# Gate tiles of a hybrid encoder block as seven block products, with stages reordered, six modulation buffers and squares in place

## The chip, the cores and the metric

The kernel runs on one core of one Trainium2 chip. The metric is the device time of one execution in microseconds (us); the median of several runs is given, and one further execution was profiled. All shares of clock and busy time below come from that profiled execution.

## The reference

One layer, 512 tokens (SEQ), model width 2048, all in float32. Cut to what matters here:

```python
mod = jax.nn.silu(c) @ w_ada[l] + b_ada[l]                 # six vectors of 2048
sh1, sc1, gt1, sh2, sc2, gt2 = jnp.split(mod, 6, axis=-1)
a = rms_norm(h, g_pre_mix[l]) * (1 + sc1) + sh1
proj = a @ w_in[l]
q, f_fw, f_bw, i_v, o_gate, z, gate_a, gate_b = jnp.split(proj, IN_SPLIT_POINTS, axis=-1)
y_a = hgrn2_bidir(q, f_fw, f_bw, i_v, o_gate, ...) @ w_a_out[l]      # 8 heads, two scans
y_b = chunked_sgu(z, g_sgu_norm[l], w_spatial[l], b_spatial[l]) @ w_b_out[l]
merged = jax.nn.sigmoid(gate_a) * y_a + jax.nn.sigmoid(gate_b) * y_b
h = h + gt1 * rms_norm(merged @ w_o[l], g_post_mix[l])
a = rms_norm(h, g_pre_ffn[l]) * (1 + sc2) + sh2
ff = jnp.square(jax.nn.relu(a @ w_ff1[l])) @ w_ff2[l]
h = h + gt2 * rms_norm(ff, g_post_ffn[l])
```

gate_a and gate_b are 2048 columns each: 16 tiles of 128 columns each, 32 gate tiles together.

## The kernel before

**Precision.** Every float32 factor is split into a high part (a cast to fp32r on ScalarE, L174) and a low part (source minus high on VectorE, L175), and a product of two such factors is the sum of three matmuls, high by high, low by high, high by low (`mm3`, L194 to L197). A tile of 128 output columns over the model width (`proj_fm`) is thus 16 x 3 = 48 matmuls of 512 token columns. Weights arrive as tiles of 1 MB (128 x 2048) by SP's DMA queue into a ring of three buffers named raw. Early stages split them in pieces of 512 columns (four buffers for the high and four for the low parts), later stages (from L663) in pieces of 1024 (four and three).

**Seven products.** `seven` (L246) computes two weight tiles at once by a Strassen-like scheme: tokens, model width and output columns are halved, and seven products of blocks take the place of eight. Each product has eight steps of a matmul of 512 columns (the high weight with the high and low activations side by side, L238) and one of 256 (the low weight with the high activation, L239). Sums of weight blocks are made on VectorE in the raw tiles (`plus`, L244). The activation side needs seven sets of blocks (S): a11, a12, a22 and the sums v1, w2, w3, v4. It is used for 28 pairs of w_ff1 tiles; `seven_tm` is its counterpart for w_o and w_ff2, where weights are the moving operand.

**Stages, in order.** (1) x is normalised and transposed; the rows of w_ada for sc1 and sh1 are multiplied with silu(c) (`ada_tile`, one VectorE instruction over a 1 MB tile, L295), two buffers named ada; each of the 16 activation tiles is modulated, split and used at once for the values of the scan and for q. (2) Eight heads: three `proj_fm` tiles each, then a scan (`head_scan`) with a long chain on VectorE. (3) Four gate_a tiles, the split of the scan's output, the other twelve gate_a tiles with two ada tiles each (`ada_next(2)`), then w_a_out. (4) The spatial gating unit: values (w_tm), layer norm, eight groups. (5) Sixteen gate_b tiles, written to DRAM, two ada tiles each until the 64 remaining ones are done. (6) w_b_out, with gate_b read back; the sums of blocks for w_o; w_o; norms. (7) w_ff1: eight plain tiles, then 28 pairs by `seven`. The result of a pair (tile both, slot h1) is added up, passed through relu and square in a further tile r (slot m1), combined to the sums that the next matrix needs, and written to DRAM by POOL's queue (L1062 to L1068). (8) w_ff2 by `seven_tm` over seven groups; s1 in slot m1 takes its first partial product. When sixteen ada tiles of one modulation are done, `post_gain` (L666) writes its 2048 numbers to DRAM as single elements.

**Order.** The tile framework lays out the instructions of each engine in an order of its own from the program's order, the tiles that come free and a planner's costs; each engine and each queue then works strictly in its order. A tile named by a slot (a0 to a7, m0 to m3, h0, h1, v0, v1) waits until the slot's last user is done.

## Time and profile before

| | |
|---|---|
| median of 3 runs | 2751.97 us (2747.85 to 2756.64) |
| profiled execution | 2751.59 us |
| its span | 2749.9 us |
| granted TensorE clock, mean | 0.991 of full |
| instructions | 33871 |
| read from DRAM, written | 422.15 MB, 69.75 MB |

The profile gives the busy time of each engine, waits with what ended them, and for each stretch of the span the share of the DMA engines in use and the TensorE clock that was granted. Busy times of consecutive matmuls overlap, so the time of one is better read from the distance between two events a known number of matmuls apart.

### The profile page before, as it was taken

Reading aid. Unit: us, or ns where it says so; the run is one execution under the profiler, and the core shown is the slowest. Engines: PE = TensorE matmul, PEld = TensorE weight load, DVE = VectorE, ACT = ScalarE, POOL = GpSimd, SP = SyncE. Lnnn points to the kernel's source line nnn. Section 1 sums busy time; section 2 is a strip of 40 time slices with the busy share of each in tenths; the row PEclk is TensorE's granted clock in tenths of the full one; section 3 lists DMA queues with packets and bytes.
Section 4 is the critical chain, followed back from the end, with each engine's and each line's share of the span. In section 5 each row is a group of like instructions: output and inputs, shape, how many; then the busy total and the mean of one; then the engine's idle time right before and its main releaser. Section 6 shows DMA issues by size and latency. Waiting matters only on the chain.

```text
span 2749.9 us, 33871 instructions
## 1 busy us (share of the span) xinstructions
PE 2680.5 (97%) x13392; PEld 2239.6 (81%) x13392; DVE 2042.4 (74%) x2442; ACT 1217.1 (44%) x1627; POOL 125.1 (5%) x152
## 2 busy tenths in 40 slices
PE   5999999999999999999999999999998999999998
PEld 4888788888788888878779988888887888888886
DVE  6876877756553666357897888888888888888856
ACT  5433333332222332233558656565655555555542
POOL 0000000000000000010000000000000011111110
PEclk9999999999999999999999999999999999999999
DMA  8852222247754558643345443434346677778772
GB/s 319 319 205 77 77 77 77 77 148 273 237 199 139 199 202 301 187 151 135 111 170 198 159 171 137 172 134 175 134 175 251 225 215 201 203 201 229 213 239 77
DMA packets 94927, 494.10 MB, mean 180 GB/s; under 512 B 10416, under 2 KB 12464, under 8 KB 47792
## 3 DMA queue, kind: packets, MB, share of 16 engines
q1 hardware_dynamic: 69168, 413.80, 42.2%
q0 software_dynamic: 25600, 78.14, 10.8%
q8 instruction: 105, 1.72, 0.2%
q14 instruction: 54, 0.44, 0.0%
HBM read 422.15 MB, written 69.75 MB: 179 GB/s over the span
## 4 chain that ended last, share of the span: by engine, by line
PE 52%; DVE 2%; issue 1%; ACT 1%; DMA 0%; DVEq 0%; ACTq 0%; POOLq 0%
PE ps_pair L238 13%; PE ps_pair L775 8%; PE ps_pair L776 8%; PE ps_pair L774 8%; PE ps_pair L239 7%; PE ps_pair L195 2%; PE ps_pair L197 2%; PE ps_pair L196 2%; PE ps_pair L1169 1%; PE ps_pair L1170 1%; PE ps_pair L1168 1%; DVE wl L175 0%; DVE raw L244 0%; DVE hr L1160 0%; ACT wh L174 0%
## 5 line engine op out<-in xcount | busy, mean ns | idle before, releaser
L174 ACT CAST wh<-raw 128x1024 fp32r<-128x1024 f32 (+1 forms) x896 | 765.8, 867 | 1015.0 <-PE ps_mm L197 391.1
L175 DVE TENSOR_TENSOR wl<-raw,wh 128x1024 fp32r<-128x1024 f32 (+1 forms) x896 | 875.6, 991 | 379.7 <-ACT wh L174 231.7
L196 PE MATMUL ps_mm<-a,wl 128*128 128x512 f32 x1152 | 450.9, 391 | 5.4 <-DVE wl L175 5.4
L195 PE MATMUL ps_mm<-a,wh 128*128 128x512 f32 x1152 | 454.3, 394 | 0.0
L197 PE MATMUL ps_mm<-a,wh 128*128 128x512 f32 x1152 | 453.5, 394 | 0.0
L238 PE MATMUL ps_pair<-mq,wh 128*128 128x512 f32 x896 | 317.2, 397 | 0.0
L196 PEld LDWEIGHTS ps_mm<-a,wl 128*128 128x128 f32 x1152 | 217.1, 188 | 51.3 <-DVE wl L175 6.6
L197 PEld LDWEIGHTS ps_mm<-a,wh 128*128 128x128 f32 x1152 | 216.9, 188 | 46.3 <-issue 1.9
L195 PEld LDWEIGHTS ps_mm<-a,wh 128*128 128x128 f32 x1152 | 217.1, 188 | 44.5 <-issue 1.9
L239 PE MATMUL ps_pair<-mq,wl 128*128 128x256 f32 x896 | 251.8, 281 | 0.0
L244 DVE TENSOR_TENSOR raw<-raw 128x1024 f32<-128x1024 f32 (+1 forms) x156 | 237.4, 1522 | 2.8
L295 DVE SCALAR_TENSOR_TENSOR raw<-raw,c_bc 128x2048 f32<-128x2048 f32 x64 | 146.5, 2290 | 102.0 <-DMA raw<-in_w_ada_dram 102.0
L238 PEld LDWEIGHTS ps_pair<-mq,wh 128*128 128x128 f32 x896 | 168.3, 188 | 40.8
L775 PE MATMUL ps_pair<-wl,a 128*128 128x512 f32 x432 | 170.2, 394 | 4.7 <-DVE wl L175 4.7
L774 PE MATMUL ps_pair<-wh,a 128*128 128x512 f32 x432 | 169.9, 393 | 0.5 <-ACT wh L174 0.5
L776 PE MATMUL ps_pair<-wh,a 128*128 128x512 f32 x432 | 169.7, 393 | 0.0
L239 PEld LDWEIGHTS ps_pair<-mq,wl 128*128 128x128 f32 x896 | 169.3, 189 | 0.0
L238 PE MATMUL ps_pair<-w,wh 128*128 128x512 f32 x448 | 159.6, 393 | 0.0
L239 PE MATMUL ps_pair<-w,wl 128*128 128x256 f32 x448 | 126.6, 283 | 0.0
L774 PE MATMUL ps_pair<-wh,v 128*128 128x512 f32 x288 | 112.9, 392 | 6.0 <-ACT wh L174 6.0
L774 PE MATMUL ps_pair<-wh,w 128*128 128x512 f32 x288 | 113.8, 395 | 3.1 <-ACT s L1130 2.1
L775 PE MATMUL ps_pair<-wl,w 128*128 128x512 f32 x288 | 113.8, 395 | 0.8 <-DVE wl L175 0.8
(279 smaller groups left out, 4564.8 us busy)
## 6 DMA issues: line engine op xcount, KB each, us to landing
raw<-in_w_ff_dram SPq DMA_DIRECT2D x72, 1024.0 KB, 6.3
raw<-in_w_fm_dram SPq DMA_DIRECT2D x64, 1024.0 KB, 4.8
raw<-in_w_ada_dram SPq DMA_DIRECT2D x64, 1024.0 KB, 5.5
raw<-in_w_ff2s_dram SPq DMA_DIRECT2D x56, 1024.0 KB, 7.2
ada<-in_w_ada_dram SPq DMA_DIRECT2D x32, 1024.0 KB, 7.0
comb_dram<-r POOLq DMA_DIRECT2D x28, 896.0 KB, 8.6
raw<-in_w_os_dram SPq DMA_DIRECT2D x16, 1024.0 KB, 4.8
ff_dram<-c POOLq DMA_DIRECT2D x28, 512.0 KB, 6.5
```

Of the source, the lines that this page charges most:

```text
L174: nc.scalar.copy(wh, src)
L175: nc.vector.tensor_tensor(wl, src, wh.bitcast(F32), op=ALU.subtract)
L195: nc.tensor.matmul(o, wh, ah, start=start, stop=False)
L196: nc.tensor.matmul(o, wl, ah, start=False, stop=False)
L197: nc.tensor.matmul(o, wh, al, start=False, stop=stop)
L238: nc.tensor.matmul(o, wh[:, c], s, start=start and i == 0, stop=False, skip_group_check=True)
L239: nc.tensor.matmul(o[:, 0, :], wl[:, c], s[:, 0, :], start=False, stop=stop and i == len(S) - 1, skip_group_check=True)
L244: nc.vector.tensor_tensor(a, a, b, op=ALU.add)
L295: nc.vector.scalar_tensor_tensor(raw, raw, 1.0, c_bc, op0=ALU.mult, op1=ALU.mult, accum_out=mod[:, i : i + 1])
L774: nc.tensor.matmul(o[:, sub], h, wh[:, c], start=first, stop=False, skip_group_check=True)
L775: nc.tensor.matmul(o[:, sub], h, wl[:, c], start=False, stop=False, skip_group_check=True)
L776: nc.tensor.matmul(o[:, sub], l, wh[:, c], start=False, stop=last, skip_group_check=True)
```

## The change

- Of the 32 gate tiles four stay plain; the other 28 are made as 14 pairs by `seven`, after the spatial unit, with activation sums prepared during the four plain tiles (`a_sums`). All gates are written to DRAM in pairs and read back for w_a_out and w_b_out.
- The order of stages becomes: heads (each followed by two ada tiles), values and spatial unit (two ada tiles per weight tile or group), gates, w_a_out (two ada tiles per weight tile), w_b_out. The outputs of both branches are written to DRAM and read back; silu(c) is loaded and computed a second time.
- At the start, w_ada tiles of activation tiles 1, 2, 4 and 5 go into slots a4 to a7, the others into the two buffers as before.
- The squares of w_ff1 are made in place in tile both, which alternates between slots m1 and h1; the last pair's squares are made inside w_ff2. A weight sum of 2048 columns in `seven_tm` is made in two halves.

```diff
-N_EARLY = 4
+N_GATES = 2
...
+    def split_in_place(t):
+
+        full = t[:, 1].bitcast(F32)
+        nc.scalar.copy(t[:, 0], full)
+        nc.vector.tensor_tensor(t[:, 1], full, t[:, 0].bitcast(F32), op=ALU.subtract)
...
         def modulated(k):
-            for m in (MOD_SC1, MOD_SH1):
...
+            for n, m in enumerate((MOD_SC1, MOD_SH1)):
+                if k < 6 and k % 3:
+                    t = big.tile([P, D], F32, tag=f"a{4 + 2 * (k % 3 - 1) + n}", name="ada")
+                else:
+                    t = pre.tile([P, D], F32, tag="ada", name="ada", bufs=2)
+                ada_tile(m, k, t)
...
     for h in range(NH):
         head_scan(h, *head_proj(h))
...
+        nc.gpsimd.dma_start(ya_dram[h // 2, :, h % 2], qA[h])
+        ada_next(2)
...
+    def values(n):
+        acc = [bank() for _ in range(4)]
+        for kb in range(4):
+            raw = load_raw(ins["w_tm"][2 + n, kb])
...
+            ada_next(2)
+        for tt in range(4):
+            nc.scalar.activation(vb[n][:, tt], acc[tt], AF.Gelu)
+
+    values(0)
...
-    with tc.tile_pool(name="yhl", bufs=1) as yp:
-        YH = [yp.tile([P, T], F32R, name=f"yh{h}") for h in range(NH)]
-        YL = [yp.tile([P, T], F32R, name=f"yl{h}") for h in range(NH)]
-        for h in range(NH):
-            split(qA[h], YH[h], YL[h])
-        for j in range(N_EARLY, KD):
-            gate(j, FM_GA, merged[j])
-            ada_next(2)
-        for jj in range(KD // 2):
-            for i, o in enumerate(proj_fm(ins["w_a_out"][jj], YH, YL, nk=NH)):
-                j = 2 * jj + i
-                nc.vector.tensor_tensor(merged[j], o, merged[j], op=ALU.mult)
-            ada_next()
...
             nc.vector.tensor_tensor(yB[g], yB[g], u, op=ALU.mult)
-            ada_next()
...
+            nc.gpsimd.dma_start(yb_dram[g // 2, :, g % 2], yB[g])
+            ada_next(2)
+    yst.close()
...
+    S = {"a11": [a[:, 0] for a in A[:8]], "v1": [a[:, 1] for a in A[:8]]}
+    S["a12"], S["a22"] = ([a[:, n] for a in A[8:]] for n in range(2))
+    kept_sums = {n: [slot(f"m{i}", (4, 2, NT), n, F32R) for i in at] for n, at in (("w2", (0, 1)), ("w3", (2, 3)))}
+    kept_sums["v4"] = [xpool.tile([P, 4, 2, NT], F32R, name=f"v4{i}") for i in range(2)]
+    for n, ts in kept_sums.items():
+        S[n] = [t[:, k] for t in ts for k in range(4)]
...
+        def a_sums():
+            for i in range(4):
+                t = gp.tile([P, 4, 2, NT], F32, tag="t", name="t", bufs=1)
+                for n, (src, hf) in enumerate(((A_of[i], 0), (A_of[i], 1), (A_of[i + 4], 1), (A_of[i + 4], 0))):
+                    nc.vector.tensor_tensor(
+                        t[:, n], src[:, :, hf, 0].bitcast(F32), src[:, :, hf, 1].bitcast(F32), op=ALU.add
+                    )
+                yield
+                nc.vector.tensor_tensor(v1[:, i], t[:, 1], t[:, 2], op=ALU.subtract)
+                nc.vector.tensor_tensor(t[:, 1], t[:, 0], t[:, 1], op=ALU.subtract)
+                nc.vector.tensor_tensor(t[:, 0], v1[:, i], t[:, 0], op=ALU.subtract)
+                nc.vector.tensor_tensor(t[:, 3], t[:, 3], t[:, 0], op=ALU.add)
+                yield
+                for name, n in (("w2", 0), ("w3", 1), ("v4", 3)):
+                    hi_lo(kept_sums[name][i // 2][:, 2 * (i % 2) : 2 * (i % 2) + 2], t[:, n])
+                    yield
+
+        steps = a_sums()
+        for j in range(2 * N_GATES):
+            (o,) = proj_fm(ins["w_fm"][FM_GA + j], AH, AL)
             sg = gp.tile([P, T], F32, tag="gate", name="gate")
-            gate(j, FM_GB, sg)
...
+            nc.scalar.activation(sg, o, AF.Sigmoid)
+            nc.gpsimd.dma_start(gate_dram[j // 2, :, j % 2], sg)
+            advance(steps, 5)
+        advance(steps, 99)
+        for i in range(4):
+            hi_lo(A_of[i][:, :, 1], v1[:, i])
...
+    rawx_stack = ExitStack()
+    rawx = rawx_stack.enter_context(tc.tile_pool(name="rawx", bufs=1))
+    raw_ring += [raw_ring[0], raw_ring[0], (rawx, "rawx")]
+    with tc.tile_pool(name="evg", bufs=1, reuse_waits="tile") as ev:
+        for p in range(N_GATES, KD):
+            n = FM_GA + 2 * p
+            both = ev.tile([P, 4, 2, NT], F32, tag="both", name="both")
+            seven(ins["w_fm"][n], ins["w_fm"][n + 1], S, ev, both, 1, 0)
+            r = ev.tile([P, 4, NT], F32, tag="r", name="r", bufs=2)
+            nc.vector.tensor_tensor(r, both[:, :, 0], both[:, :, 1], op=ALU.add)
+            nc.scalar.activation(r, r, AF.Sigmoid)
+            nc.gpsimd.dma_start(gate_dram[p].rearrange("p n t -> p (n t)"), r.rearrange("p n t -> p (n t)"))
+    raw_ring = raw_ring[:1]
+    rawx_stack.close()
+    x_stack.close()
...
+    def load_y(t, src):
+        nc.gpsimd.dma_start(t[:, 1].bitcast(F32), src)
+        split_in_place(t)
+        return t
...
+    with tc.tile_pool(name="c2", bufs=1) as c2:
+        YH, YL = parts_of_y([load_y(slot(f"a{i}", (2, 2, T), f"ya{i}", F32R), ya_dram[i]) for i in range(4)])
+        c_bc = c2.tile([P, D], F32, name="c_bc2")
+        nc.sync.dma_start(c_bc, ins["c"].broadcast_to([P, D]))
+        cs = slot("a7", (D,), "cs")
+        nc.scalar.activation(cs, c_bc, AF.Sigmoid)
+        nc.vector.tensor_tensor(c_bc, c_bc, cs, op=ALU.mult)
...
+        def load_ga():
+            if len(ga) < 4:
+                ga.append(slot(f"a{4 + len(ga)}", (2, 2, T), "ga"))
+                nc.gpsimd.dma_start(
+                    ga[-1].rearrange("p n i t -> p n (i t)"),
+                    gate_dram[2 * len(ga) - 2 : 2 * len(ga)].rearrange("n p i t -> p n (i t)"),
+                )
...
+        for jj in range(KD // 2):
+            if jj % 2 == 0:
+                load_ga()
+            for i, o in enumerate(proj_fm(ins["w_a_out"][jj], YH, YL, nk=NH)):
+                j = 2 * jj + i
+                nc.vector.tensor_tensor(merged[j], o, ga[j // 4][:, j // 2 % 2, j % 2], op=ALU.mult)
+            ada_next(2)
+            if jj >= 4:
+                i = jj - 4
+                yb.append(load_y(yp.tile([P, 2, 2, T], F32R, name=f"yb{i}"), yb_dram[i]))
+        YH, YL = parts_of_y(yb)
...
-                plus(b11, b12)
+                for c in (slice(0, WIDE), slice(WIDE, 2048)):
+                    plus(b11[:, c], b12[:, c])
...
+    def squares(p, both):
+
+        a, b = both[:, :, 0], both[:, :, 1]
+        nc.vector.tensor_tensor(a, a, b, op=ALU.add)
+        nc.scalar.activation(a, a, AF.Relu)
+        nc.scalar.activation(a, a, AF.Square)
+        nc.vector.tensor_tensor(b[:, 0:2], a[:, 0:2], a[:, 3::-3], op=ALU.subtract)
+        nc.vector.tensor_tensor(b[:, 2], b[:, 0], a[:, 1], op=ALU.subtract)
+        nc.vector.tensor_tensor(b[:, 3], b[:, 2], a[:, 2], op=ALU.add)
+        for t, n in ((a[:, 1:4], 0), (b, 3)):
+            nc.gpsimd.dma_start(
+                comb_dram[p // 4, n : n + t.shape[1], :, p % 4].rearrange("s p c -> p s c"), t
+            )
+
     with tc.tile_pool(name="ev", bufs=1, reuse_waits="tile") as ev:
         for p in range(4 * FF_GROUPS):
             n = N_PLAIN + 2 * p
-            r = slot("m1", (8, NT), "r")
-            both = slot("h1", (4, 2, NT), "both")
+            both = slot("h1" if p % 2 else "m1", (4, 2, NT), "both")
             seven(ins["w_ff1"][n], ins["w_ff1"][n + 1], S, ev, both)
-            if p == 4 * FF_GROUPS - 1:
-                for name in SETS:
-                    next_set(0, name)
-                for _ in range(3):
-                    split_set(lambda i: i)
-            w2, v4 = r[:, 6], r[:, 7]
-            nc.vector.tensor_tensor(r[:, 0:4], both[:, :, 0], both[:, :, 1], op=ALU.add)
-            nc.scalar.activation(r[:, 0:4], r[:, 0:4], AF.Relu)
-            nc.scalar.activation(r[:, 0:4], r[:, 0:4], AF.Square)
-            nc.vector.tensor_tensor(r[:, 4:6], r[:, 0:2], r[:, 3::-3], op=ALU.subtract)
-            nc.vector.tensor_tensor(w2, r[:, 4], r[:, 1], op=ALU.subtract)
-            nc.vector.tensor_tensor(v4, w2, r[:, 2], op=ALU.add)
-            nc.gpsimd.dma_start(comb_dram[p // 4, :, :, p % 4].rearrange("s p c -> p s c"), r[:, 1:8])
+            if p < 4 * FF_GROUPS - 1:
+                squares(p, both)
+        for name in SETS:
+            next_set(0, name)
+        for _ in range(3):
+            split_set(lambda i: i)
+
...
+                if g == 0 and u == 0 and name == "w3":
+                    squares(4 * FF_GROUPS - 1, both)
                 if u == 0:
```

## Rows read from the trace of the kernel before

**Rows 1.** The page: span, and busy us, share of the span and instructions by engine.

```profile
span 2749.9 us, 33871 instructions
...
PE 2680.5 (97%) x13392; PEld 2239.6 (81%) x13392; DVE 2042.4 (74%) x2442; ACT 1217.1 (44%) x1627; POOL 125.1 (5%) x152
```

**Rows 2.** Windows: stretch, length, busy by engine, granted clock, DMA share, GB/s.

```profile
25.00:30.00 5.00, 2.09 (x19) 1.79 (x17) 5.00 (x6) 4.22 (x9) 0.00 (x0) 1.00 0.33 93
...
272.00:569.00 297.00, 297.00 (x1797) 239.21 (x1796) 225.92 (x428) 98.34 (x161) 0.00 (x0) 1.00 0.21 75
...
1020.00:1110.00 90.00, 90.00 (x398) 74.54 (x397) 58.31 (x68) 25.98 (x43) 4.35 (x8) 1.00 0.82 294
...
1600.00:1700.00 100.00, 100.00 (x571) 87.20 (x570) 87.75 (x92) 56.00 (x66) 4.88 (x5) 1.00 0.42 156
...
2095.00:2105.00 10.00, 10.00 (x54) 8.58 (x53) 9.81 (x9) 3.10 (x4) 0.00 (x0) 1.00 1.03 426
```

**Rows 3.** Evictions by line: count, ns min/median/max, first and last start, forms.

```profile
L562 ACT ACTIVATE gate<-ps_mm x16: 597/599/604, 1022.0 to 1185.2; 128x512 f32<-128x512 f32 x16
...
L276 ACT COPY both<-ps_pair x28: 587/587/590, 1569.2 to 2101.6; 128x512 f32<-128x512 f32 x28
...
L555 DVE SCALAR_TENSOR_TENSOR q<-ps_hg,g_hgrn,og x8: 749/750/751, 272.1 to 568.4; 128x512 f32<-128x512 f32 x8
...
L282 DVE TENSOR_TENSOR q<-ps_mm,q x24: 676/685/692, 114.7 to 220.5; 128x512 f32<-128x512 f32 x24
```

**Rows 4.** Waits in three stretches: engine, tile, releaser: total, times, longest.

```profile
PE ps_pair L195 <- ACT wh L174: 2.1, 2, 1.6
...
PEld ps_hg L510 <- DVE qv L493: 1.7, 7, 0.2
...
SPq L294 <- DVE ada L295: 52.1, 13, 9.5
```

**Rows 5.** Groups by line and form: count, busy us, mean ns, idle before.

```profile
L175 DVE TENSOR_TENSOR wl<-raw,wh 128x1024 fp32r<-128x1024 f32 x180 | 215.1, 1219 | 1.2 <-ACT wh L174 0.3
L174 ACT CAST wh<-raw 128x1024 fp32r<-128x1024 f32 x180 | 184.3, 1052 | 189.5 <-DVE raw L244 159.2 <-PE ps_pair L238 30.3
...
L244 DVE TENSOR_TENSOR raw<-raw 128x1024 f32<-128x1024 f32 x103 | 125.8, 1221 | 1.7
...
L295 DVE SCALAR_TENSOR_TENSOR raw<-raw,c_bc 128x2048 f32<-128x2048 f32 x16 | 36.7, 2291 | 21.1 <-DMA raw<-in_w_ada_dram 21.1
L175 DVE TENSOR_TENSOR wl<-raw,wh 128x512 fp32r<-128x512 f32 x53 | 35.9, 689 | 51.7 <-ACT wh L174 51.7
```

**Rows 6.** Timeline of ScalarE in the first gate tiles: start, us, line.

```profile
689.65 0.60 ACT L562 ACTIVATE mg<-ps_mm 128x512 f32<-128x512 f32 x1 [2.10 <-PE ps_mm L197]
...
701.87 1.14 ACT L174 CAST wh<-raw 128x512 fp32r<-128x512 f32 x2 [11.11 <-DMA raw<-in_w_fm_dram]
...
707.29 0.60 ACT L562 ACTIVATE mg<-ps_mm 128x512 f32<-128x512 f32 x1 [2.33 <-PE ps_mm L197]
...
719.90 0.60 ACT L562 ACTIVATE mg<-ps_mm 128x512 f32<-128x512 f32 x1 [2.10 <-PE ps_mm L197]
```

**Rows 7.** DMA issues in both gate stretches: KB each, median us to landing.

```profile
pg_dram<-pg POOLq DMA_DIRECT2D x1, 8.0 KB, 13.6
...
raw<-in_w_ada_dram SPq DMA_DIRECT2D x16, 1024.0 KB, 6.3
```

**Rows 8.** Timeline of ScalarE at the start: first and fourth activation tile.

```profile
31.82 0.62 ACT L217 CAST a<-xT 128x512 fp32r<-128x512 f32 x1
...
58.90 0.62 ACT L217 CAST a<-xT 128x512 fp32r<-128x512 f32 x1
```

**Rows 9.** Timeline from w_ff1 to w_ff2.

```profile
2106.85 0.39 PE L774 MATMUL ps_pair<-wh,v 128*128 128x512 f32 x1
...
2120.60 1.01 ACT L1130 COPY s<-ps_pair 128x1024 f32<-128x1024 f32 x1 [1.92 <-DMA comb_dram<-r]
...
2121.67 0.79 PE L774 MATMUL ps_pair<-wh,w 128*128 128x512 f32 x1 [2.14 <-ACT s L1130]
```

More of the change, by code (lines that the diff above doesn't have):

```diff
@@ L218, in split, with hi_lo, advance, acts @@
         nc.vector.tensor_tensor(L, src, H.bitcast(F32), op=ALU.subtract)
-    def acts():
-        pairs = [big.tile([P, 2, 2, 2, 256], F32R, tag=f"a{i}", name=f"a{i}") for i in range(KD // 2)]
+    def hi_lo(dst, src):
+        nc.scalar.copy(dst[:, :, 0], src)
+        nc.vector.tensor_tensor(dst[:, :, 1], src, dst[:, :, 0].bitcast(F32), op=ALU.subtract)
+    def split_in_place(t):
+        full = t[:, 1].bitcast(F32)
+        nc.scalar.copy(t[:, 0], full)
+        nc.vector.tensor_tensor(t[:, 1], full, t[:, 0].bitcast(F32), op=ALU.subtract)
+    def advance(steps, n):
+        for _ in range(n):
+            if next(steps, True):
+                break
+    def acts(at):
+        pairs = [big.tile([P, 2, 2, 2, 256], F32R, tag=f"a{i}", name=f"a{i}") for i in at]
         return pairs, [t[:, n] for t in pairs for n in range(2)]
@@ L345 @@
                         nc.scalar.copy(x, o)
-        A = acts()[1]
+        A_of, A = acts(range(4))
         AH, AL = highs(A), lows(A)
         def modulated(k):
-            for m in (MOD_SC1, MOD_SH1):
-                ada_tile(m, k, pre.tile([P, D], F32, tag="ada", name="ada", bufs=2))
+            if k == KD // 2:
+                more = acts(range(4, KD // 2))
+                A_of.extend(more[0])
+                A.extend(more[1])
+                AH.extend(highs(more[1]))
+                AL.extend(lows(more[1]))
+            for n, m in enumerate((MOD_SC1, MOD_SH1)):
[4 more added lines that the diff above has]
+                ada_tile(m, k, t)
             nc.vector.tensor_scalar(
@@ L410, in slot @@
         return pool.tile([P, *shape], dtype, tag=at, name=name)
-    mg = [slot("m0", (4, T), "mg0")]
-    merged = [mg[0][:, n] for n in range(4)]
     atd = []
@@ L591 @@
         nc.sync.dma_start(bsp, ins["b_spatial"].partition_broadcast(P))
-        vb = sp.tile([P, 4, 1024], F32, name="vb")
-        for n in range(2):
-            acc = [bank() for _ in range(4)]
-            for kb in range(4):
-                raw = load_raw(ins["w_tm"][2 + n, kb])
-                for off, wh, wl in halves(raw):
-                    for kk in range(STEP // 512):
-                        k = 4 * kb + off // 512 + kk
-                        w = slice(kk * 512, (kk + 1) * 512)
-                        for tt in range(4):
-                            mm_tm(acc[tt], k, tt, wh[:, w], wl[:, w], k == 0, k == KD - 1)
-            for tt in range(4):
-                nc.scalar.activation(vb[:, tt, n * 512 : (n + 1) * 512], acc[tt], AF.Gelu)
-            ada_next(2)
+        values(1)
         for tt in range(4):
@@ L640 @@
             nc.vector.tensor_tensor(yB[g], yB[g], u, op=ALU.mult)
-            ada_next()
-    gate_dram = dram.tile([KD, P, T], F32, name="gate_dram")
-    yst2 = ExitStack()
-    yp = yst2.enter_context(tc.tile_pool(name="yhl2", bufs=1, side="right"))
-    YH = [yp.tile([P, T], F32R, name=f"yh{h}") for h in range(NH)]
-    YL = [yp.tile([P, T], F32R, name=f"yl{h}") for h in range(NH)]
-    for h in range(NH):
-        split(yB[h], YH[h], YL[h])
-    with tc.tile_pool(name="gates", bufs=2) as gp:
-        for j in range(KD):
-            sg = gp.tile([P, T], F32, tag="gate", name="gate")
-            gate(j, FM_GB, sg)
-            nc.gpsimd.dma_start(gate_dram[j], sg)
-            ada_next(2)
@@ L666, in post_gain @@
+    assert not ada_rest
     def post_gain(m, g):
@@ L710, in as_set @@
         return [t[:, i] for i in range(4)]
-    def advance(steps, n):
-        for _ in range(n):
-            if next(steps, True):
-                break
     sets = {}
@@ L735, in load_gate @@
             if len(sgs) < KD:
-                t = bp.tile([P, T], F32, tag="sg", name="sg", bufs=4)
-                nc.gpsimd.dma_start(t, gate_dram[len(sgs)])
-                sgs.append(t)
-        for j in range(4):
+                t = bp.tile([P, 2, T], F32, tag="sg", name="sg", bufs=2)
+                nc.gpsimd.dma_start(t, gate_dram[KD // 2 + len(sgs) // 2])
+                sgs.extend((t[:, 0], t[:, 1]))
+        for j in range(2):
             load_gate()
```

58 lines of the change are left out of this document (35 added, 23 removed).

## The prediction

> **What bounds the kernel now.** I read the page's engine shares first, then busy time by stretch, then who waited for whom, and last the timeline wherever something waited. TensorE is busy 2680.5 of 2749.9 us, so it is the bound; VectorE comes second with 74% [rows 1]. The stretches are to be read with granted clock and DMA share beside the busy time: in the heads TensorE has no idle time at 76% VectorE, in the gate tiles none at 65% VectorE and 0.82 DMA share, in the paired block products of the feed-forward none at 87% VectorE [rows 2]. So a gain can only come from fewer TensorE columns or from the few places where TensorE stands still. There are three larger ones: the start, one place inside the first gate tiles, and the change from the first to the second feed-forward matrix. Matmul busy times overlap (0.39 us each in the page, one per 0.227 us in time), so I take costs from the distance between evictions. The profiled execution took 2751.59 us, 0.4 below the median of the runs; its span is 2749.90, with 1.7 us around it. The sum is made against 2751.6.
>
> **1. Gate tiles as seven block products.** The second set of sixteen gate tiles evicts from 1022.0 to 1185.2, fifteen steps: 163.2/15 = 10.88 us a tile, or 10.88/48 = 0.2267 us a matmul of 512 columns. The same seven-product routine in the feed-forward evicts 28 pairs from 1569.2 to 2101.6: 532.4/27 = 19.72 us a pair [rows 3]. Fourteen pairs of gate tiles take that form and four tiles stay plain: 14 x (2 x 10.88 - 19.72) = 14 x 2.04 = **28.6 us saved**. The pairs' VectorE work is that of the feed-forward pairs less two 256-column and one 512-column subtraction, so the cover (87% there, TensorE never idle) holds; ScalarE gets one sigmoid of 1024 columns for relu and square. If a 0.5 us wait came back in each pair the saving would be 21.6.
> Seven products replace 96 loads of weights and 96 x 512 columns by 112 loads and 56 x 768 columns: 12.5% fewer columns, but 19.72 against 21.76 is 9.4% less time, so the 256-column matmul costs 0.352 - 0.227 = 0.125 us and not half of 0.227 [rows 3]. The Trainium skill (TensorE: Matmul & The Clock Gate, section Back-to-back issue gap) gives 262 and 518 cycles for 256 and 512 columns. An estimate from that page would be 18.2 us a pair, 20.7 for two plain tiles, 35 us saved in all and a sum of 2712; the trace shows both forms to be slower, so its rows are used.
>
> **2. The change of stage.** Today the smaller staging tiles give way to the larger ones between gates and w_b_out: TensorE waits twice for the first casts, 2.1 us in all [rows 4]. This goes from there and comes back ahead of the pairs, where it is longer: a product of a pair is 19.72/7 = 2.8 us, while addition, cast and subtraction of its weights are 1.22 + 1.05 + 1.22 = 3.5 us in a row [rows 5], with nothing prepared ahead for the first few products. The sums of activation blocks fall under the four plain tiles: per part eight 512-column operations and three splits, 11 x 0.69 = 7.6 us of VectorE, four times, beside 2.8 us of weight splits per tile: 10.4 of 10.88 us. That barely hides; without this cover it is up to 30 us of VectorE, of which I expect almost nothing on the path. Net **+3 us** (-2 to +8).
>
> **3. Entry to w_a_out.** Its activations now come back from DRAM. The slots come free after the second product of the last pair, 5 x 2.8 = 14 us before its end; four loads of 0.5 MB and a cast plus subtraction (2.3 us) for the first of them fit in that time. What is queued behind a late split on VectorE is the weights' subtraction, for which TensorE waits. **+3 us** (0 to 8).
>
> **4. Modulation tiles moved.** Of 64 modulation tiles 16 go into the heads, 16 into the values, 16 into the spatial groups, 16 into w_a_out; each is 1 MB on SP's queue and 2.29 us of VectorE [rows 5]. Values and groups get the density that the second gate set has today (three tiles of 1 MB per 10.88 us) without TensorE idle [rows 2]. In a head (296.3/7 = 42.3 us) two tiles add 4.6 us to a VectorE with 24% x 42.3 = 10 us idle [rows 2, 3], but the scan's second attention product starts right when its VectorE input arrives: its weight loads waited for it seven times, by at most 0.2 us [rows 4]. A modulation tile placed ahead of that chain pushes it. **+3 us** for eight heads (0 to 8 x 2.3 = 18).
> In w_a_out the traffic becomes 8 weight tiles, 16 modulation tiles, 4 MB of gates and 2 MB of the other branch: 30 x 1.05 = 31.5 MB in 8 x 10.88 = 87 us, 361 GB/s. The dense gates show 294 GB/s at share 0.82, so 359 at full share; the most I see is 426 [rows 2]. By these it needs 74 to 88 us, by 294 it would be 107. **+4 us** (0 to 20).
>
> **5. The scattered 8 KB rows.** When the sixteenth tile of a modulation is done, POOL writes its 2048 numbers to DRAM. It landed 13.6 us after its issue, the weight tile loaded beside it kept ScalarE waiting 11.1 us, and two gates took 17.64 and 12.61 instead of 10.88: 8.5 us [rows 6, 7]. After the change the same write falls at the end of the heads, where the next weights (values) are due. I let 6 of the 8.5 come back: **-2.5 us** (-8.5 to 0). The second such row today falls where few loads follow; then it meets the first w_b_out loads: **+1** (0 to 8.5).
>
> **6. Six modulation buffers at the start.** With two buffers SP's queue waited 52 us in the first 100 for VectorE to free them; DMA stood at 0.33 share from 25 to 30 us [rows 2, 4]. The first activation tile is cast at 31.8, the fourth at 58.9; from the end of that first cast at 32.4 there are 768 matmuls of 0.2267 us (24 for each of 16 activation tiles, 384 for q), due to end at 206.5, and the last q eviction is at 220.5: 14.0 us lost [rows 3, 8]. With loads ready, VectorE sets the pace: 2 x 2.29 + 0.42 + 3 x 0.69 = 7.1 us per tile, the fourth at 31.8 + 21.3 = 53.1, **6 us earlier** (0 to -14.0; 0 if loads of the next tiles now queue behind the transposes that free a4 to a7).
>
> **7. Squares in place, double buffered, the last ones put off.** Steady pairs have no TensorE wait, so nothing is gained there; one more POOL issue of 1 us per pair is hidden. But at the end the slot m1 of the squares is wanted for the first partial result of w_ff2: the copy starts at 2120.60 on the landing of their write to DRAM, and the third product starts at 2121.67, where 24 matmuls after 2106.85 it could have at 2112.3 [rows 9]. That is 9.4 us; a granted clock below full comes on top. Now m1 holds the last but one pair, written 20 us before. **-9.4 us** (-10.6 to -5, the weight additions being next in line). Halving the 2.29 us addition lets the cast start 1.1 us sooner at the few entries where TensorE waits for it: **-1** (-3 to 0).
>
> Sum: -28.6 + 3 + 3 + 3 + 4 - 2.5 + 1 - 6 - 9.4 - 1 = -33.5; 2751.6 - 33.5 = **2718 us**.
>
> **Rivals.** (B) *Transfers and late chains eat half.* w_a_out is held to 294 GB/s (16 us beyond the sum), the scattered rows cost 8.5 each (10 beyond), the entries 8 each (10 beyond); half of these 36 us gives 2736, all of them 2754. For it: 361 GB/s asked in one stage; against: the loads on POOL can run before they are needed. The Trainium skill (DMA: Bandwidth & Descriptors, section Queues, rings and completion order) has the 16 engines take turns between queues by packet, which speaks against a free ride for POOL's loads beside SP's; no row here separates the two. (C) *Slower: the heads become bound by VectorE's order.* If both modulation tiles stand before the second direction's chain and wait for their loads (6.3 us to landing in the dense stage [rows 7]), each head grows by 2 x 2.3 + 1.5 = 6 us and more; it decides from (33.5 + 8.3)/8 = 5.2 us a head. At 7 us: 2718 + 8 x 7 - 3 = 2771. Against: ring slots are freed 10.88 us apart, so loads are early. (D) *All stalls go.* No scattered-row stall, no new entries, 10 us at the start: with 5 us left for all else: -28.6 - 8.5 - 10 - 10.6 - 2 + 5 = -55, 2697. (E) *The pairs save nothing*, as w_fm pairs run slower than w_ff1's: 2718 + 28.6 = 2747, no change; same routine, same shapes speak against.
>
> **How the numbers follow.** A difference below 0.3% (8.3 us) can't be told from none. Forecast 0.68, B 0.16, C 0.06, D 0.08, E 0.02. The forecast's own range is 2705 to 2731; adding most of B and part of D gives 2702 to 2738. Faster is the forecast, D and most of B: 0.89; same is E and B's end: 0.05; slower is C: 0.06.
>
> **What would show it.** Gate pairs 19.7 us apart at their last copies; no wait between 2106 and 2122's counterpart; the fourth activation cast near 53; w_a_out tiles 10.9 us apart. Wrong if pairs are over 20.5 apart, if heads exceed 43.5 us, or if TensorE waits over 10 us in w_a_out.

## The result, and the profile after

The changed kernel takes 2715.91 us in the median of four runs (2708.53 to 2718.85) against 2753.14 us for the kernel before (four runs, 2747.85 to 2756.64): ratio 0.9862, 95% interval 0.9836 to 0.9888, 37 us less. The forecast was 2718. The profiled execution of the changed kernel is the shortest of its four (2708.53 us), so the two traces stand 43.1 us apart and not 37; the account below is made between the traces.

The page of the changed kernel, its span and busy us by engine, answers to [rows 1]:

```profile
span 2706.8 us, 34621 instructions
...
PE 2645.1 (98%) x13616; PEld 2221.9 (82%) x13616; DVE 2215.1 (82%) x2587; ACT 1283.2 (47%) x1649; POOL 152.7 (6%) x202
```

TensorE is busy 35 us less and still bounds the kernel; VectorE has gone from 74% to 82%. Evictions and sigmoids by line (count, ns min/median/max, first and last start) answer to [rows 3]: last q of the projection, heads, gate pairs, w_a_out; and the fourth activation cast from ScalarE's timeline answers to [rows 8]:

```profile
L302 DVE TENSOR_TENSOR q<-ps_mm,q x24: 677/688/692, 105.7 to 211.8; 128x512 f32<-128x512 f32 x24
...
L583 DVE SCALAR_TENSOR_TENSOR q<-ps_hg,g_hgrn,og x8: 743/746/749, 265.9 to 571.8; 128x512 f32<-128x512 f32 x8
...
L715 ACT ACTIVATE r<-r x14: 1052/1056/1063, 809.0 to 1065.8; 128x1024 f32<-128x1024 f32 x14
...
L758 DVE TENSOR_TENSOR mg<-ps_pair,ga x16: 681/686/693, 1070.3 to 1158.0; 128x512 f32<-128x512 f32 x16
...
53.00 0.62 ACT L222 CAST a<-xT 128x512 fp32r<-128x512 f32 x1
```

The reader sees: the last q comes at 211.8 in place of 220.5, the fourth cast at 53.00 (forecast 53.1); the fourteen pairs stand 256.8/13 = 19.75 us apart (forecast 19.72); w_a_out's last merge is 92.2 us after the last pair's sigmoid. TensorE's waits over the whole trace, those above 1.5 us (total, times, longest):

```profile
PE ps_mm L360 <- DVE xtok L355: 17.4, 2, 16.7
PE ps_mm L333 <- ACT a L222: 6.9, 2, 5.4
PE ps_pair L866 <- DVE wl L180: 6.5, 4, 3.9
PE ps_pair L200 <- ACT wh L179: 3.3, 1, 3.3
PE ps_mm L333 <- DVE og L473: 3.3, 1, 3.3
PE ps_pair L865 <- ACT wh L179: 2.7, 3, 1.4
PE ps_pair L201 <- DVE wl L180: 2.5, 2, 1.5
PE ps_pair L259 <- DVE wl L180: 1.9, 3, 0.8
PE ps_pair L258 <- ACT wh L179: 1.6, 1, 1.6
```

L360 is the transposing of x at the start (17.1 us in the kernel before), L258 and L259 are the first pair's products, L200 and L201 of ps_pair are w_a_out, L473 is the end of the last head, and L865 and L866 are the products of w_o and w_ff2; of these last only 1.6 us fall at the change from w_ff1 to w_ff2, where ScalarE's copy into m1 now follows its neighbours without a wait, against [rows 9]:

```profile
2071.72 1.06 ACT L1147 ACTIVATE both<-both 128x1024 f32<-128x1024 f32 x1
2072.69 1.00 ACT L1231 COPY s<-ps_pair 128x1024 f32<-128x1024 f32 x1
```

The largest new stall is in w_a_out. Four windows of 2 us (busy by engine as in [rows 2], granted clock, DMA share, GB/s), and ScalarE's timeline ahead of them:

```profile
1071.58 2.01 ACT L179 CAST wh<-raw 128x1024 fp32r<-128x1024 f32 x2 [4.69 <-DMA raw<-in_w_a_out_dram]
1081.79 1.05 ACT L232 CAST yb<-yb 128x1024 fp32r<-128x1024 f32 x1 [8.19 <-DMA yb<-yb_dram]
1086.65 1.04 ACT L232 CAST yb<-yb 128x1024 fp32r<-128x1024 f32 x1 [3.81 <-DMA yb<-yb_dram]
1087.60 1.99 ACT L179 CAST wh<-raw 128x1024 fp32r<-128x1024 f32 x2
...
1086.00:1088.00 2.00, 0.00 (x0) 0.00 (x0) 1.19 (x4) 1.35 (x2) 0.00 (x0) 1.00 1.02 418
1088.00:1090.00 2.00, 0.49 (x1) 0.19 (x1) 2.00 (x2) 1.59 (x2) 0.00 (x0) 0.98 1.04 418
1090.00:1092.00 2.00, 1.86 (x4) 1.50 (x5) 2.00 (x4) 0.00 (x0) 0.00 (x0) 0.50 1.03 422
1092.00:1094.00 2.00, 2.00 (x7) 1.58 (x6) 2.00 (x2) 0.00 (x0) 0.00 (x0) 0.67 1.03 410
```

TensorE stands still (3.3 us, then 0.95 more), then runs on at a granted clock of 0.50 and 0.67. The time at the lower level of 1.2 GHz is 2.0 + 2 x 0.33/0.5 = 3.3 us, half of it lost: this stall of some 4 us cost up to 1.7 more. In its timeline matmuls start 0.43 us apart there (1091.16, 1091.58, 1092.01) and 0.23 apart outside. The Trainium skill (TensorE: Matmul & The Clock Gate, section HAM oscillation — how this bites in real kernels) counts the same half of the throttled time as the price behind a wait; this trace agrees.

### The profile page after: what moved, and what is told of

It is laid out like the page before. It is cut to its first block, busy times and chain, and to the rows that moved or that the text cites. A ratio compares the mean times of both kernels' runs of the same rounds, so it can differ in the third digit from the quotient of the medians.

```text
span 2706.8 us, 34621 instructions
## 1 busy us (share of the span) xinstructions
PE 2645.1 (98%) x13616; PEld 2221.9 (82%) x13616; DVE 2215.1 (82%) x2587; ACT 1283.2 (47%) x1649; POOL 152.7 (6%) x202
## 4 chain that ended last, share of the span: by engine, by line
PE 56%; DVE 3%; ACT 1%; issue 1%; DMA 1%; DVEq 0%; POOL 0%; ACTq 0%
PE ps_pair L258 13%; PE ps_pair L866 8%; PE ps_pair L867 8%; PE ps_pair L865 8%; PE ps_pair L259 7%; PE ps_pair L201 3%; PE ps_pair L202 3%; PE ps_pair L200 3%; PE ps_pair L1270 1%; PE ps_pair L1271 1%; PE ps_pair L1269 1%; DVE wl L180 1%; DVE raw L264 1%; DMA yb<-yb_dram 0%; DVE hr L1261 0%
## 5 line engine op out<-in xcount | busy, mean ns | idle before, releaser
L258 PE MATMUL ps_pair<-mq,wh 128*128 128x512 f32 x896 | 317.2, 397 | 0.0
L264 DVE TENSOR_TENSOR raw<-raw 128x1024 f32<-128x1024 f32 (+1 forms) x223 | 307.2, 1379 | 3.4
L200 PE MATMUL ps_mm<-a,wh 128*128 128x512 f32 x704 | 279.2, 397 | 0.0
L201 PE MATMUL ps_mm<-a,wl 128*128 128x512 f32 x704 | 277.4, 394 | 0.0
L202 PE MATMUL ps_mm<-a,wh 128*128 128x512 f32 x704 | 275.1, 391 | 0.0
L259 PE MATMUL ps_pair<-mq,wl 128*128 128x256 f32 x896 | 251.8, 281 | 0.0
L258 PE MATMUL ps_pair<-w,wh 128*128 128x512 f32 x672 | 239.2, 393 | 0.0
L258 PEld LDWEIGHTS ps_pair<-mq,wh 128*128 128x128 f32 x896 | 168.3, 188 | 40.8
L259 PE MATMUL ps_pair<-w,wl 128*128 128x256 f32 x672 | 190.0, 283 | 0.6 <-DVE wl L180 0.6
L866 PE MATMUL ps_pair<-wl,a 128*128 128x512 f32 x432 | 169.6, 392 | 4.7 <-DVE wl L180 4.7
L865 PE MATMUL ps_pair<-wh,a 128*128 128x512 f32 x432 | 169.5, 392 | 0.0
L259 PEld LDWEIGHTS ps_pair<-mq,wl 128*128 128x128 f32 x896 | 169.3, 189 | 0.0
L258 PE MATMUL ps_pair<-a,wh 128*128 128x512 f32 x448 | 159.0, 399 | 1.6 <-ACT wh L179 1.6
L202 PEld LDWEIGHTS ps_mm<-a,wh 128*128 128x128 f32 x704 | 132.2, 188 | 28.6 <-issue 1.4
L201 PEld LDWEIGHTS ps_mm<-a,wl 128*128 128x128 f32 x704 | 132.3, 188 | 28.4 <-issue 2.9
L200 PEld LDWEIGHTS ps_mm<-a,wh 128*128 128x128 f32 x704 | 132.4, 188 | 25.8 <-issue 0.6
L258 PEld LDWEIGHTS ps_pair<-w,wh 128*128 128x128 f32 x672 | 126.2, 188 | 29.0
L259 PE MATMUL ps_pair<-a,wl 128*128 128x256 f32 x448 | 126.0, 281 | 1.4 <-DVE wl L180 1.4
```

Source lines behind the costliest of these rows:

```text
L200: nc.tensor.matmul(o, wh, ah, start=start, stop=False)
L201: nc.tensor.matmul(o, wl, ah, start=False, stop=False)
L202: nc.tensor.matmul(o, wh, al, start=False, stop=stop)
L258: nc.tensor.matmul(o, wh[:, c], s, start=start and i == 0, stop=False, skip_group_check=True)
L259: nc.tensor.matmul(o[:, 0, :], wl[:, c], s[:, 0, :], start=False, stop=stop and i == len(S) - 1, skip_group_check=True)
L264: nc.vector.tensor_tensor(a, a, b, op=ALU.add)
```

## The experiments

Three questions: which part of the gain belongs to which part of the change, what holds w_a_out, and how much the heads bear. Each kernel is the changed one with the edit shown, timed against the kernel before on the same chip; e9 to e12 share a chip, as do e1 to e4 and e5 to e8.

**The changed kernel again (e9).** No edit.

> The changed kernel once more, without an edit, on the same chip as the next three: it is what they are compared with. Both theories expect a ratio to the kernel before of 0.984 to 0.989.

Ratio 0.9866 (0.9848 to 0.9884), 2713.08 us. The span of its trace is 2711.8 us, 5.0 more than the first, with TensorE's waits the same to within 1.1 us in every row above; the mean granted clock is 0.992 and not 0.995. So 3 to 5 us between two traces of different kernels say nothing unless a row names them.

**Six modulation buffers undone (e1).**

```diff
-                if k < 6 and k % 3:
+                if False:
```

> The changed kernel with two modulation buffers at the start, as before the change. If the six buffers are what brought the last q eviction from 220.5 to 211.8 us, it comes back to 220 to 221, the fourth activation cast to 58 to 59, and the time rises by about 8.7 us, to 2725. Rival, the start was held by the transfers' rate and gained from something else in the change (the order of slots, the activations taken in two halves): the last q eviction stays at 211 to 213 and the time within 2 us of the changed kernel's.

Ratio 0.9908 (0.9891 to 0.9924), 2723.73 us. The last q by line:

```profile
L302 DVE TENSOR_TENSOR q<-ps_mm,q x24: 677/686/692, 114.1 to 220.4; 128x512 f32<-128x512 f32 x24
```

220.4 against 211.8: 8.6 of the start's 8.7 us are the buffers'. The last q of the other traces with six buffers comes between 211.3 and 213.6, so the size is known to some 2 us. The rival falls. By the ratios the kernel lost 12 us; the 3 beyond the start are no more than the spread that e9 shows.

**Squares as before (e2).** The separate slot m1 for the squares, one slot h1 for the products, the last pair squared ahead of w_ff2.

```diff
-            both = slot("h1" if p % 2 else "m1", (4, 2, NT), "both")
+            r = slot("m1", (8, NT), "r")
+            both = slot("h1", (4, 2, NT), "both")
...
-                if g == 0 and u == 0 and name == "w3":
-                    squares(4 * FF_GROUPS - 1, both)
...
```

> The changed kernel with the squares as before the change: a slot of their own (m1), one slot for the products (h1), the last pair squared ahead of w_ff2. If the late write to DRAM out of m1 was the whole wait, the stretch from the last copy of the first feed-forward matrix to the end goes from 639.8 back to about 648.3 us, with a copy waiting for that write and TensorE standing 9 us in the third product; the time rises by 8.5 us, to about 2724. Rival, the halved addition or the entry's order gave that gain: the stretch stays within 2 us of 639.8.

Ratio 0.9901 (0.9883 to 0.9918), 2721.54 us. TensorE's wait at the change to w_ff2 and ScalarE's copy ahead of it:

```profile
PE ps_pair L865 <- ACT s L1237: 7.7, 1, 7.7
...
2090.63 1.01 ACT L1237 COPY s<-ps_pair 128x1024 f32<-128x1024 f32 x1 [4.00 <-DMA comb_dram<-r]
```

The wait on the landing of the last write is back as in [rows 9], and the stretch from the last copy (2072.0) to the end (2720.6) takes 648.6 us, against 639.8 and 641.5 in the two traces of the changed kernel: 7 to 9 us. The rival falls, and the wait is that for the late write; which of the three parts that were undone together removes it was not separated.

**The halved addition undone (e12).**

```diff
-                for c in (slice(0, WIDE), slice(WIDE, 2048)):
-                    plus(b11[:, c], b12[:, c])
+                plus(b11, b12)
```

> The changed kernel with the first addition of a set of w_o and w_ff2 products whole again (one of 2048 columns, 2.29 us, in place of two halves). If the halves let the casts at the entries of w_o and w_ff2 start 1.1 us sooner, TensorE's waits there grow by 1 to 3 us in all and the time by as much, which the medians hardly show. Rival, the addition is covered everywhere: the waits of TensorE after 1250 us stay within 0.5 us of what they are.

Ratio 0.9878 (0.9863 to 0.9894), 2715.84 us, 2.8 over e9 with overlapping intervals. TensorE's waits in the products of w_o and w_ff2, which were 6.5 and 2.7:

```profile
PE ps_pair L866 <- DVE wl L180: 8.5, 6, 3.9
PE ps_pair L865 <- ACT wh L179: 2.4, 2, 1.4
```

1.7 us more in all, most of it at the entry of w_ff2. The waits grow as the theory says, but no stretch shows the time: from the last merge of w_b_out to the last copy of w_ff1 it is 820.7 us (820.4 and 822.1 in the two traces of the changed kernel), from there to the end 641.6 (639.8 and 641.5). What the halves are worth stays open.

**All gate tiles plain (e3).**

```diff
-N_GATES = 2
+N_GATES = 16
```

> The changed kernel with all 32 gate tiles plain, none by seven products (the sums of activation blocks are still made, beside the first plain tiles). If a pair saves 2 x 10.88 - 19.75 = 2.01 us and nothing else hangs on it, the fourteen give 28.1 us back and the slow start of the first pair (4.5 us) goes, while the change to the larger staging tiles falls on w_a_out (2 to 5 us): 24 to 28 us more, 2740 to 2744. Rival, the seven products also brought the stall of w_a_out, whose late activations and other loads come only after the last pair: that goes too, and the time rises by 15 to 19 us only.

Ratio 0.9987 (0.9977 to 0.9998), 2747.16 us: 33 us more than the changed kernel's ratio, not 24 to 28, and not 15 to 19. The gates by line, TensorE's waits from 1085 to 1125 us, and a window there:

```profile
L693 ACT ACTIVATE gate<-ps_mm x32: 590/598/599, 754.2 to 1092.6; 128x512 f32<-128x512 f32 x32
...
PE ps_pair L201 <- DVE wl L180: 6.1, 1, 6.1
PE ps_pair L200 <- ACT wh L179: 5.0, 3, 4.3
...
1112.00:1116.00 4.00, 0.47 (x1) 0.47 (x2) 4.00 (x5) 0.00 (x0) 0.00 (x0) 0.54 1.03 424
```

The gates stand 338.4/31 = 10.92 us apart, so the price of the pairs themselves is about as forecast, 28 to 29 us. On top, w_a_out is entered worse and not better: 11.1 us of waits, and the clock at half behind two of them. Part of that is the experiment's own: it still splits the unused activation sums into the slots a0 to a3 behind the last plain tile, and the loads of w_a_out's activations wait for that (issued from 1081.8 us on, 10.8 before the last gate's sigmoid; in the changed kernel from 1045.9, 19.9 before). So the rival, a stall of w_a_out brought by the pairs, isn't borne out, but a run that delays the activations itself can't refute it either; e6 below speaks against it, where the pairs stay and the stall goes. How much of the 5 us on top would belong to a kernel without that delay stays open.

**The yb casts behind the weight casts (e4).** The first theory of the stall in w_a_out: a load that came early in program terms blocks ScalarE's queue.

```diff
-        nc.scalar.copy(t[:, 0], full)
+        pin(nc.scalar.copy(t[:, 0], full))
...
-                yb.append(load_y(yp.tile([P, 2, 2, T], F32R, name=f"yb{i}"), yb_dram[i]))
+                yb.append(load_y(yp.tile([P, 2, 2, T], F32R, name=f"yb{i}"), yb_dram[i], tc.keep_in_program_order))
```

> The changed kernel with the four casts and subtractions that split the other branch's activations (yb) kept behind the weight casts of the w_a_out tile they are written with, instead of ahead of them in ScalarE's queue; the loads themselves are issued as before. If ScalarE's queue is what holds w_a_out (a yb cast waits 8.2 us for its load and the weight casts stand behind it), TensorE's waits of 3.3 and 2.5 us there go, the eight tiles take 87 to 91 us from the last pair's copy in place of 96.1, and the time falls by 5 to 8 us, to 2708 to 2711. Rival, the transfers hold it (DMA share 1.01 from 1070 to 1100 us): the weight casts then wait for their own loads, the stage keeps 94 to 97 us and the time stays within 2 us.

Ratio 0.9864 (0.9847 to 0.9880), 2711.71 us: no gain. ScalarE's timeline where the yb casts stood:

```profile
1088.28 1.99 ACT L179 CAST wh<-raw 128x1024 fp32r<-128x1024 f32 x2 [15.87 <-DMA raw<-in_w_a_out_dram]
```

The weight cast of the third tile starts no earlier (1087.60 before): its own load is late as well. The wait for yb that the profile names ahead of it was not what held it. The theory falls.

**The yb loads on SP's queue (e5).** They are issued there behind the weights of tiles 2 to 5.

```diff
...
-            if jj >= 4:
-                i = jj - 4
-                yb.append(load_y(yp.tile([P, 2, 2, T], F32R, name=f"yb{i}"), yb_dram[i]))
+            if 2 <= jj < 6:
+                i = jj - 2
+                yb.append(load_y(yp.tile([P, 2, 2, T], F32R, name=f"yb{i}"), yb_dram[i], False))
+            if jj >= 4:
+                split_in_place(yb[jj - 4], tc.keep_in_program_order)
```

> The changed kernel with the four loads of the other branch's activations (yb, 0.5 MB each) on SP's queue, behind the w_a_out loads of tiles 2 to 5, in place of POOL's queue, where they run ahead to the start of w_a_out; their casts stay behind the weight casts of tiles 4 to 7. With the casts alone put back, the second w_a_out weight tile still came late: its cast waited 15.9 us for its load while DMA stood at 1.02 share, 421 GB/s. If loads that POOL issues too early are what crowds it out, TensorE's waits of some 6 us at 1080 to 1092 go or halve and the time falls by 3 to 6 us, to 2708 to 2711. Rival, the total asked of w_a_out is too much wherever it stands (30 MB in 87 us), or the ring slots that the modulation tiles hold delay the weight load: the waits stay at 5 to 7 us and the time within 2 us.

Ratio 0.9856 (0.9831 to 0.9881), 2709.00 us; TensorE's waits in w_a_out stay:

```profile
PE ps_pair L200 <- ACT wh L179: 3.0, 1, 3.0
PE ps_pair L201 <- DVE wl L180: 2.5, 2, 1.8
```

So POOL's early loads of yb don't hold it either: the third weight tile is still issued at 1076.5 us and cast at 1087.4, while the first load of yb is now issued at 1087.4. The four gate loads of 1 MB, which POOL issues around the start of this stage, were moved in no run.

**Half of the modulation bytes (e10).**

```diff
+        h = slice(0, D // 2)
+        nc.sync.dma_start(raw[:, h], ins["w_ada"][i][:, h])
+        for _ in range(2):
+            nc.vector.scalar_tensor_tensor(
+                raw[:, h], raw[:, h], 1.0, c_bc[:, h], op0=ALU.mult, op1=ALU.mult, accum_out=mod[:, i : i + 1]
+            )
...
```

> The changed kernel, in which the sixteen modulation tiles of w_a_out load only half of their bytes (512 KB) and VectorE works twice on that half, so that the tiles take the same slots in the same order and about the same VectorE time, and 8 MB less is transferred; the other half of those sixteen products is left out. If w_a_out is held by the rate of its transfers (1.02 share from 1070 to 1100 us), the second weight tile lands in time, TensorE's waits of 3.3 and 2.5 us go, and the stage falls by 5 to 7 us as it does with eight tiles moved to the heads. Rival, the three slots shared by weights and modulation tiles hold it (the weight load is issued only at 1076.4 us, when VectorE has freed a slot): the load is issued no earlier, TensorE still waits 3 us or more, and the stage gains under 2 us.

Ratio 0.9853 (0.9838 to 0.9869), 2709.49 us. SP's issue of the third weight tile, the cast that waits for it, and the window between them:

```profile
1078.88 0.33 SPq L196 DMA_DIRECT2D raw<-in_w_a_out_dram  x1
...
1089.04 1.99 ACT L179 CAST wh<-raw 128x1024 fp32r<-128x1024 f32 x2 [2.66 <-DMA raw<-in_w_a_out_dram]
...
1080.00:1090.00 10.00, 7.87 (x35) 6.19 (x33) 6.49 (x10) 3.08 (x4) 0.00 (x0) 1.00 1.03 417
```

TensorE still waits 4.9 us (6.1 in e9), and from the last pair's sigmoid to the last merge the stage takes 91.1 us (92.5 in e9): under 2 us gained, as the rival has it. The DMA engines are still full here, and the load is issued as late relative to the last pair's sigmoid as without the edit (10.6 us after it in both). That speaks for the place of the weight load in SP's queue. It doesn't clear the transfers: of the 8 MB only 2 stand ahead of the late tile in that queue, and POOL's gates and activations come as before.

**Three modulation tiles a head, one a w_a_out tile (e6).**

The first call stands beside a head, the second beside a w_a_out tile.

```diff
-        ada_next(2)
+        ada_next(3)
...
-            ada_next(2)
+            ada_next()
```

> The changed kernel with three modulation tiles beside each head in place of two, and one beside each w_a_out tile in place of two: 8 MB of loads and 18 us of VectorE move from w_a_out to the heads. If w_a_out is held by its transfers and the heads have room (VectorE 85% of 42.33 us, 6.2 us idle, one tile more takes 2.3), the heads stay at 42.3 to 42.6 us each and TensorE's waits in w_a_out go: 5 to 6 us less, 2709 to 2711; the row of 8 KB then goes out inside the sixth head instead of the last, with a stall of the same 4 to 8 us. Rival, the heads' VectorE chain bears no third tile: each head grows by 1 to 2.3 us, 8 to 18 us in all, and the time rises by 3 to 12 us.

Ratio 0.9835 (0.9816 to 0.9853), **2702.75 us**: 8 us under the changed kernel by the ratios (its interval and e9's just overlap) and 6 to 7 under e5 and e7 on the same chip, the best version found with e8. A window of its heads (VectorE has 187.15 there in the changed kernel), SP's issues of the third and fourth w_a_out tile, the cast of the third, TensorE's waits there, the merges, and the window of the former stall:

```profile
300.00:520.00 220.00, 219.87 (x1330) 175.67 (x1329) 197.00 (x346) 72.67 (x118) 3.90 (x6) 1.00 0.44 153
...
1069.82 0.33 SPq L196 DMA_DIRECT2D raw<-in_w_a_out_dram  x1
1072.59 0.33 SPq L196 DMA_DIRECT2D raw<-in_w_ada_dram  x1
1074.80 0.33 SPq L196 DMA_DIRECT2D raw<-in_w_a_out_dram  x1
...
1079.40 2.00 ACT L179 CAST wh<-raw 128x1024 fp32r<-128x1024 f32 x2 [11.88 <-DMA raw<-in_w_a_out_dram]
...
PE ps_pair L201 <- DVE wl L180: 1.8, 2, 1.1
...
L758 DVE TENSOR_TENSOR mg<-ps_pair,ga x16: 682/684/686, 1069.7 to 1152.2; 128x512 f32<-128x512 f32 x16
...
1080.00:1090.00 10.00, 10.00 (x46) 8.29 (x45) 5.22 (x6) 4.46 (x5) 0.00 (x0) 1.00 0.95 385
```

The last merge comes 85.7 us after the last pair's sigmoid (92.2 before). The third weight tile, which was issued at 1076.4 us behind two modulation tiles, each waiting for a slot of the shared ring that VectorE frees, is now issued at 1069.8 behind one. It is no quicker (9.6 us from issue to cast, 10.2 in e10), the DMA engines are nearly as full as before (0.95), and TensorE doesn't wait, since the cast comes 8 us earlier. The heads stay whole at 90% VectorE: from the projection's last q to the first gate's sigmoid it takes 539.0 us, against 540.7 and 539.9 in the two traces of the changed kernel.

**Four tiles a head, none in w_a_out (e11).** As e6, with `ada_next(4)` and no call in w_a_out.

> The changed kernel with four modulation tiles beside each head and none in w_a_out. If VectorE's share decides the heads, they stretch now: two tiles leave 85% of 42.33 us, a third adds 2.3 us (it cost the eight heads under 2 us in all), a fourth makes 40.6 of 42.3 us, 96%, and the scan's chains wait behind it: 1 to 3 us a head, 8 to 24 in all, against a gain in w_a_out of 6 to 7 us: 2712 to 2735. Rival, the order leaves room to the last: heads at 42.3 to 42.6 us, 2701 to 2705.

Ratio 0.9944 (0.9930 to 0.9957), 2733.98 us. TensorE's wait in the heads, and the first gates:

```profile
PE ps_hg L538 <- DVE qv L521: 20.0, 6, 5.6
...
L693 ACT ACTIVATE gate<-ps_mm x4: 592/595/597, 780.7 to 808.7; 128x512 f32<-128x512 f32 x4
```

This is rival C's mechanism, the attention product of the scan waiting for VectorE's input: the very wait of [rows 4], at most 0.2 us there, is up to 5.6 us long. It sets in between the third and the fourth tile: from the projection's last q (213.2) to the first gate's sigmoid it now takes 567.5 us, 27 more than with two tiles and above the 8 to 24 that were expected.

**The scattered rows written as lines (e7).** TensorE turns the [128, 16] tile first, so that 16 lines of 512 bytes go out, after w_a_out and w_b_out.

```diff
...
-        nc.gpsimd.dma_start(row.rearrange("o (k p) -> p (o k)", p=P), t)
+        nc.tensor.transpose(turned, t, ident)
+        nc.vector.tensor_copy(lines, turned)
+        nc.gpsimd.dma_start(row.rearrange("o (k p) -> (o k) p", p=P), lines)
...
```

> The changed kernel with the two rows of 2048 numbers turned by TensorE first and written to DRAM as 16 lines of 512 bytes, after w_a_out and after w_b_out, in place of 2048 numbers of 4 bytes each, the first of them inside the last head. If the scattered write is what delays the modulation tile and the values' weights beside it, the last head and the change to the values lose their stall (the last head's period of 51.9 us falls to 42 to 47) and the time falls by 4 to 6 us, to 2710 to 2712. Rival, the last head is long for want of other work, with the row only beside it: no change within 2 us.

Ratio 0.9855 (0.9835 to 0.9875), 2709.97 us: within the interval of no change. The heads by line, and the entry of the pairs (window from 770 to 800 us):

```profile
L583 DVE SCALAR_TENSOR_TENSOR q<-ps_hg,g_hgrn,og x8: 745/748/750, 265.9 to 567.9; 128x512 f32<-128x512 f32 x8
...
770.00:800.00 30.00, 27.62 (x132) 23.12 (x131) 25.05 (x30) 13.14 (x17) 0.54 (x1) 0.89 0.41 147
```

The last head ends 3.9 us earlier and its wait for og is gone, so the write of the row is the cause of that stall; its place and its form were changed together. But the end of w_a_out (1157.8 against 1158.0) is where it was. Of the 3.8 us by which the first gate's sigmoid comes earlier, 1.0 is gone by the first pair's, where the granted clock is 0.89 and the first trace shows 1.00 for the same window (e9's shows 0.89 as well); 0.9 more goes over the pairs, and 1.7 in w_a_out, where TensorE waits 6.6 us here and 5.8 there. A local gain of 4 us is shown; that it reaches the end is not.

**The three edits together (e8).** e5, e6 and e7 in one kernel.

> The changed kernel with the three edits together: yb loads on SP's queue behind the weights, three modulation tiles a head and one a w_a_out tile, and the two rows written as lines. If the stalls are separate, the gains add: 5 to 6 us in w_a_out (the first two edits remove the same one) and 4.7 us at the end of the heads, 2704 to 2707. Rival, a third tile slows the heads: 2712 to 2722.

Ratio 0.9834 (0.9817 to 0.9852), 2703.24 us: the same as e6 alone. The row written as lines adds nothing there, since with three tiles a head, in e6, the scattered row already goes out at 435.7 us, inside a head, where TensorE's waits in all the heads come to 0.4 us.

## Why the prediction was right, by its own steps

The forecast of 2718 and the range from 2702 to 2738 held. Term by term, forecast against the traces (negative is time saved):

| step | forecast | measured | from |
|---|---|---|---|
| 1 gate pairs | -28.6 | -28.1 | 19.75 us a pair; e3 |
| 2 change of stage, with 5's second row | +3 +1 | 0 | first pair 4.5 over its 19.75, w_b_out 4.4 shorter |
| 3, 4 w_a_out | +3 +4 | +9.1 | 96.1 from the last pair's copy to the last merge, less 87.0 |
| 4 modulation tiles in heads | +3 | 0 | the first seven q 42.33 us apart as before |
| 5 first scattered row | -2.5 | -4.6 | 8.5 left the gates, 3.9 came back at the heads' end; e7 |
| 6 six buffers | -6 | -8.7 | last q; e1 |
| 7 squares | -9.4 | -8.5 | last copy to the end; e2 |
| 7 halved addition, and the rest | -1 | -3 | from w_b_out's end to w_ff1's (-1.3 with e9's trace); e12 gives no time to the halves |

The sum of the middle column is -33.5, of the measured one -43.8, against 43.1 between the traces; 0.7 has no row. Against the medians (37) the forecast is nearer than against the traces, since the profiled execution was the shortest. That it came within 2 us of the median is in part luck: five of the eight rows were too cautious by 2 to 4 us, all on the same side.

The large terms stood on distances between evictions of the same routine, and these held to 0.03 us a pair. The prediction's estimate from the Trainium skill (TensorE: Matmul & The Clock Gate, section Back-to-back issue gap), by that page's gap of a single matmul, would have given 35 us for step 1; the trace gives 28.1.

What was off: step 6 by 2.7 us, since only the fourth cast was priced, while what the projection gains goes on to the last q. Step 4's heads were too dear: two tiles cost nothing, nor does a third (e6); rival C's mechanism exists, but shows with the fourth (e11). Step 2 was too dear by some 4: w_b_out gave back as much as the pairs' start took. In w_a_out the size was nearly right (9.1 for 7) by luck, for the reason was right in part at most: step 3 named VectorE's late split and step 4 the rate of the transfers. e4 and e5 show that neither the order of the casts nor POOL's early loads of yb matter, e10 that half of the modulation bytes helps little, and e6 that fewer modulation tiles do. What is left is the weight load's place in SP's queue, behind modulation tiles whose slots VectorE has to free: where 10 us pass from issue to cast while DMA is full, an issue 7 us later is a stall. The rate has a part in it, since a gate's weight tile lands in 4.9 us (median of the trace). e6 shows the issue moved and the time to the cast not; but it takes bytes and VectorE's work out of the stage too. Neither the issue alone nor POOL's gate loads were moved in a run of their own, so this cause is argued and not shown.

Of the 36 us that rival B could lose only the 2.1 in w_a_out appeared; the first row cost 3.9 where 6 were allowed. Rival D failed at w_a_out and the first pair, rival E on the pairs' 19.75 us. Of the signs, the pairs, the fourth cast and the 5.8 us of waits in w_a_out came as stated; 1.6 us of waits stayed at the change to w_ff2, and the tiles of w_a_out did not stand 10.9 us apart at the stall. The last head's 51.9 us (519.9 to 571.8) is over the 43.5 that was to be a sign of error: 3.9 of it is the row, and without the row (e7) it is still 48.1 with 0.2 us of waits, so the rest is other TensorE work that now comes between and no loss.

## What to carry to other kernels

Price a routine by the distance of its evictions elsewhere in the same trace, not by its matmul count: 12.5% fewer columns were 9.2% less time (19.75 for 21.76 us). Before moving side work into a stage, look at the share of the engine that will do it and at the queue its loads share with the stage's weights; at 90% VectorE the heads bore it, though not a tile more; at 8 weight tiles behind 16 others in a ring of three w_a_out did not. When the profile blames one wait, move that one alone first: the blame on yb fell here in two runs.
